# The sample tokens' products with their states: one fp32 product, or two fp32r products over high and low parts

## The chip, the cores and the metric

The kernel runs on one core of one Trainium2 chip. The metric is the device time of one execution in microseconds (us). Engines are named as in the profile: PE (matmul) with its weight loads PEld, DVE (VectorE), ACT (ScalarE), POOL (GpSimd) and SP (SyncE, which issues nearly all DMAs).

## The reference

One inference step of a decoder layer for a prompt of 1024 tokens and for 8 sample tokens, each with its own state. An input projection feeds a gated short convolution (branch A) and a gated delta rule with 8 heads (branch B); both are projected, gated, merged and projected again. What the change touches is the delta rule for the sample tokens, one token for each of 8 samples and 8 heads, with a 128 x 128 state:

```python
Per token: S = a_t S; S = S + beta_t k_t (v_t - k_t^T S); o_t = q_t^T S.
# written for one token, with S the state before it:
r = beta * (v - a * (k^T S))          # k, q are l2-normalised
o = a * (q^T S) + (q^T k) * r
S_new = a * S + k r^T
```

So each head needs k^T S and q^T S for 8 samples: 8 states as weights, each with 2 columns (k and q) that stream past.

## The kernel before

Activations lie with channels on partitions; the 1024 prompt tokens and the 8 sample tokens are 1032 columns, in three groups of 344. A job is one block of 128 output channels of a projection: 3 groups x 8 blocks of the contraction x 3 products. Its operands are fp32 numbers split into a high and a low part of the type fp32r (`xh`, `xl`, `whi`, `wlo`), and high x high, high x low and low x high are summed, each in one pass. `split(hi, lo, src)` makes such parts: a copy on ACT that rounds, and a subtraction on DVE. A head has 6 jobs: k, q, v, two gates, z.

Beside the jobs run strands, written as Python generators: for each head a delta rule over the prompt in 8 chunks (`delta_gen`), and one for the samples (`sample_gen`). A planner (`Sched`) keeps a clock for each engine from assumed costs. After each block of three main products, `slot()` lets every strand whose time has come write its next instructions, up to its next `yield`. So the order on every engine's queue is fixed when the kernel is built; at run time each engine takes its queue in that order and waits where data is missing. PE's queue is main products with the strands' small products strewn in.

In the state chain of `delta_gen`, chunk after chunk, PE forms products with the state S (`S,kq`), DVE forms X from them, PE multiplies (`X,U`), ACT copies the result as `vn`, PE forms `vn,kd`, and DVE adds that to S.

`sample_gen(h)` starts at the first job of head h + 1. It takes slots of 4 KB a partition from `T4` (six of them, shared with other strands and jobs; `T4.ready(n)` asks for n free ones, `T4.get` takes one, `T4.give` returns it), loads the 8 states of the head as `s0` (a DMA of 512 KB on SP's queue), forms the norms of k and q, multiplies the states with k and q, forms r and o, writes r to HBM and reads it back spread over all partitions (`rB`), forms the new states in place and stores them. The trace names the tile of the states S, as it does the state of the chain; `qs_s` holds k and q of all heads and samples.

Of the kernel before, what the change touches and what calls it, by code (L numbers as in the profile page):

```python
# [9 lines left out]
F32R = mybir.dt.float32r  # L10
I32 = mybir.dt.int32
AF = mybir.ActivationFunctionType
ALU = mybir.AluOpType
# [3 lines left out]
P = 128  # L17
D = 1024
NK = 8
S = 1024  # L20
NB = 8
NT = S + NB
NH = 8
C = 128
# [129 lines left out]
def hybrid_step(  # L154
# [9 lines left out]
    V, A, PE, GP, SY = (Paced(e, n, sched) for e, n in (  # L164
        (nc.vector, "V"), (nc.scalar, "A"), (nc.tensor, "PE"), (nc.gpsimd, "GP"), (nc.sync, "SY")))
# [9 lines left out]
    def ps_aux():  # L175
        return psum["pa"].tile([P, 512], F32, tag="pa", name="pa_t")

    def tt(out, a, b, op):
        V.tensor_tensor(out=out, in0=a, in1=b, op=op)

    def ts(out, a, s1, s2=None, op0=ALU.mult, op1=None):
        if s2 is None:
            V.tensor_scalar(out=out, in0=a, scalar1=s1, scalar2=None, op0=op0)
        else:
            V.tensor_scalar(out=out, in0=a, scalar1=s1, scalar2=s2, op0=op0, op1=op1)

    def stt(out, a, s, b, op0, op1):
        V.scalar_tensor_tensor(out=out, in0=a, scalar=s, in1=b, op0=op0, op1=op1)

    def store(out, in_):  # L190
        sched.loose()
        SY.dma_start(out=out, in_=in_)
        sched.loose(False)

    def act(out, in_, func, **kw):
        A.activation(out=out, in_=in_, func=func, **kw)

    def split(hi, lo, src):
        A.copy(out=hi, in_=src)
        tt(lo, src, hi.bitcast(F32), ALU.subtract)  # L200

    def rsqrt(pool, x, n, w, name, tag=""):
        y = pool.tile([P, w], F32, tag=f"rs_y{w}{tag}", name=f"{name}_y")[:n]
        a = pool.tile([P, w], F32, tag=f"rs_a{w}", name=f"{name}_a")[:n]
        ts(y.bitcast(I32), x.bitcast(I32), -0.5, 1597463007.0, ALU.mult, ALU.add)
        for _ in range(3):
            tt(a, y, y, ALU.mult)
            stt(a, a, -0.5, x, ALU.mult, ALU.mult)
            stt(y, a, 1.5, y, ALU.add, ALU.mult)
        return y  # L210
# [49 lines left out]
    qs_s = cpool.tile([P, NH, NB, 2], F32, name="qs_s")  # L260
# [5 lines left out]
    smp = dram.tile([2, NB, NH], F32, name="smp")  # L266
# [10 lines left out]
    def transpose(out, in_):  # L277
        n = in_.shape[0]
        PE.transpose(out, in_, ident[:n, :n])
# [385 lines left out]
    def when(*conds):  # L665
        while not all(c() for c in conds):
            yield
# [124 lines left out]
    flags = {}  # L792
# [413 lines left out]


    def sample_gen(h):
        while not flags.get(("qs", h)) or (h and not flags.get(("smp", h - 1))) or not T4.ready(2):
            yield  # L1210
        sm = lambda name, w=NB: bp.tile([P, w], F32, tag=f"sm_{name}", name=f"sm_{name}")
        s0_, rB_ = T4.get("S0", S), T4.get("rB", S)
        s0 = s0_.rearrange("p (b e) -> p b e", e=C)
        SY.dma_start(out=s0, in_=state_delta[0, :, h].rearrange("b d e -> d b e"))
        kk, qq = qs_s[:, h, :, 0], qs_s[:, h, :, 1]
        prod = sm("prod", 3 * NB).rearrange("p (a b) -> p a b", b=NB)
        tt(prod[:, 0], kk, kk, ALU.mult)
        tt(prod[:, 1], qq, qq, ALU.mult)
        tt(prod[:, 2], kk, qq, ALU.mult)
        yield  # L1220
        pt = ps_aux()
        PE.matmul(pt[:, 0:3 * NB], lhsT=ones, rhs=prod.rearrange("p a b -> p (a b)"), start=True, stop=True)
        s2 = sm("s2", 2 * NB)
        ts(s2, pt[:, 0:2 * NB], EPS, op0=ALU.add)
        qk = sm("qk")
        V.tensor_copy(out=qk, in_=pt[:, 2 * NB:3 * NB])
        rr = rsqrt(bp, s2, P, 2 * NB, "rsk")
        rk_, rq_ = rr[:, 0:NB], rr[:, NB:2 * NB]
        ts(rq_, rq_, C ** -0.5)
        eg_, be_ = gbs[:, 0, :, h], gbs[:, 1, :, h]  # L1230
        ks, fk, fq, egs = sm("ks"), sm("fk"), sm("fq"), sm("egs")
        tt(ks, kk, rk_, ALU.mult)
        tt(fk, rk_, eg_, ALU.mult)
        tt(fq, rq_, eg_, ALU.mult)
        tt(qk, qk, rk_, ALU.mult)
        tt(qk, qk, rq_, ALU.mult)
        V.tensor_copy(out=egs, in_=eg_)
        yield
        pq = ps_aux()
        for b in range(NB):  # L1240
            PE.matmul(pq[:, 2 * b:2 * b + 2], lhsT=s0[:, b, :], rhs=qs_s[:, h, b, :], start=True, stop=True)
            if b % 4 == 3:
                yield
        pqv = pq[:, 0:2 * NB].rearrange("p (n t) -> p n t", t=2)
        r, t_ = sm("r"), sm("t")
        o_ = os_all[:, h, :]
        tt(r, pqv[:, :, 0], fk, ALU.mult)
        tt(r, v_s[:, h, :], r, ALU.subtract)
        tt(r, r, be_, ALU.mult)
        tt(o_, pqv[:, :, 1], fq, ALU.mult)  # L1250
        tt(t_, qk, r, ALU.mult)
        tt(o_, o_, t_, ALU.add)
        yield

        sched.cur.t += 4000.0
        yield
        pt = ps_aux()
        transpose(pt[:NB, 0:P], r)
        rT = bp.tile([NB, P], F32, tag="sm_rT", name="sm_rT")
        V.tensor_copy(out=rT, in_=pt[:NB, 0:P])  # L1260
        SY.dma_start(out=rsc[h], in_=rT)
        rB = rB_.rearrange("p (b e) -> p b e", e=C)
        SY.dma_start(out=rB, in_=rsc[h].unsqueeze(0).to_broadcast([P, NB, C]))
        yield
        for b in range(NB):
            act(rB[:, b, :], rB[:, b, :], AF.Copy, scale=ks[:, b:b + 1])
            stt(s0[:, b, :], s0[:, b, :], egs[:, b:b + 1], rB[:, b, :], ALU.mult, ALU.add)
            if b % 2:
                yield
        store(n_delta_s[0, :, h].rearrange("b d e -> d b e"), s0)  # L1270
        T4.give(s0_)
        T4.give(rB_)
        flags["smp", h] = True
# [85 lines left out]
    for h in range(NH):  # L1359
        i0 = len(jobs)  # L1360
        st_h = head_jobs(h)
        if h:
            hook(i0, lambda h=h: start(sample_gen(h - 1)))
        for g in gates[2 * h:2 * h + 2]:
            gate_job(*g)
        zb_job(h, st_h)
# [3 lines left out]
    for t in range(SG):  # L1370
        branch_a_jobs(t)
    hook(iga, lambda: (start(sample_gen(NH - 1)), start(sample_norm_gen()), start(conv_state_gen("b"))))


# [8 lines left out]
    def alloc(key, side):  # L1383
        pools[key] = tc.alloc_tile_pool(name=key, bufs=1, side=side)
        return pools[key]
# [369 lines left out]
    T4 = Slots(alloc("t4", "left"), "t4", NT4, CY)  # L1755
    bp = tc.alloc_tile_pool(name="bpool", bufs=1, side="left")
# [67 lines left out]
    for j in range(9):  # L1824
        i, n, xr, mh, ml, held = pre.pop(j)
# [33 lines left out]
        for half in range(2):  # L1859
            hs = slice(half * 512, (half + 1) * 512)  # L1860
            stt(yt[:n, hs], yt[:n, hs], r, xr[:n, hs], ALU.mult, ALU.add)
            out = y_prompt[0, i * P:(i + 1) * P, hs] if i < 8 else y_sample[:, 0, hs]
# [38 lines left out]
```

## Time and profile before

| | |
|---|---|
| median of 3 runs | 1423.75 us (1422.88 to 1424.92) |
| profiled execution | 1422.29 us, span 1420.6 us |
| busy in the span | PE 1396.6, PEld 1341.2, DVE 937.7, ACT 658.0, POOL 36.5 us |
| sample products with states | 64 in the program, 128 records in the trace, first at 147.8, last at 776.2 us |
| issue of the 8 state loads | 124.0 (head 0) to 757.6 us (head 7) |

Nearly every instruction is recorded under line L121, where a helper issues them, so groups are told apart by their tiles: `pa_t<-qs_s,S` is a product into `pa_t` with streaming operand `qs_s` and weights S. A row of the timeline has the start in us from the span's start, its length, the engine, the operation, its tiles and shapes, and the number of instructions merged in it; in brackets the idle time ahead of it and what ended it. A row of the groups has the count, then total busy us, mean ns of one, and the idle time just before. A matmul's recorded length contains its way through the array; the distance between starts tells the rate. A row of stretches has its limits, its length, then busy us (and instructions) of PE, PEld, DVE, ACT and POOL, the granted clock of PE, the busy share of the DMA engines, and GB/s.

### The profile page before, as it was taken

The page shows a single profiled execution, that of the slowest core. Times are in us where ns is not written, and L with a number is a line of the kernel's source. Part 1 is how long each engine was busy: PE and PEld are TensorE (multiplying, and loading weights), DVE is VectorE, ACT ScalarE, POOL GpSimd, SP SyncE. Part 2 cuts the span into 40 slices and gives each one's busy share as a digit, 9 for nine tenths or more (in the row PEclk, how much of TensorE's full clock was granted, in tenths as well). Part 3 has the DMA queues.
Part 4 walks back from the last instruction along what each step waited for, and adds up shares of the span by engine and source line. Part 5 has one row for each costly group of instructions (what it writes and reads, how often), then busy time and mean ns, then how long its engine had stood idle before and what let it go on. Part 6 is the DMA issues. An engine that isn't in the chain of part 4 may idle for free.

```text
span 1420.6 us, 25886 instructions
## 1 busy us (share of the span) xinstructions
PE 1396.6 (98%) x10130; PEld 1341.2 (94%) x10130; DVE 937.7 (66%) x2444; ACT 658.0 (46%) x1521; POOL 36.5 (3%) x72
## 2 busy tenths in 40 slices
PE   6999999999999999999999999999999999999997
PEld 4899999999999999999999999999999999999786
DVE  6754846758468494494764816978977857864553
ACT  6767453845529465284573332343333344532211
POOL 0000000000001000010000000000000200000000
PEclk9999999999999999999999999999999999999999
DMA  9523352233323333324232323255621875643221
GB/s 321 147 48 94 91 118 71 80 86 93 87 70 106 87 84 94 72 76 106 62 110 69 85 62 86 95 176 170 207 76 31 248 250 182 231 151 93 95 85 59
DMA packets 191396, 161.76 MB, mean 114 GB/s; under 512 B 34311, under 2 KB 166816, under 8 KB 191266
## 3 DMA queue, kind: packets, MB, share of 16 engines
q1 hardware_dynamic: 186720, 151.58, 36.3%
q0 software_dynamic: 4352, 8.46, 2.0%
q8 instruction: 79, 1.29, 0.4%
q14 instruction: 43, 0.35, 0.1%
q10 hardware_dynamic: 202, 0.08, 0.0%
HBM read 123.40 MB, written 36.91 MB: 113 GB/s over the span
## 4 chain that ended last, share of the span: by engine, by line
PE 91%; DVE 5%; DMA 3%; ACT 1%; SPq 0%; issue 0%; DVEq 0%; ACTq 0%
PE pm_t L121 66%; PE pa_t L121 22%; PE pb L121 2%; DVE kq L121 1%; DMA xs<-in_x_prompt_dram 1%; DMA yraw<-yAsc 1%; DMA wor<-in_w_o_dram 0%; DVE S L121 0%; SPq L121 0%; DMA sg<-gAsc 0%; DVE wlo L121 0%; DVE Tw L121 0%; DVE Ttmp L121 0%; DMA sg<-gBsc 0%; DVE ml L121 0%
## 5 line engine op out<-in xcount | busy, mean ns | idle before, releaser
L121 PE MATMUL pm_t<-xh,whi 128*128 128x344 f32 (+1 forms) x1576 | 520.1, 330 | 0.0
L121 PE MATMUL pm_t<-xl,whi 128*128 128x344 f32 (+1 forms) x1576 | 498.1, 316 | 0.0
L121 PE MATMUL pm_t<-xh,wlo 128*128 128x344 f32 (+1 forms) x1576 | 498.1, 316 | 0.0
L121 PEld LDWEIGHTS pm_t<-xh,whi 128*128 128x128 f32 x1576 | 297.0, 188 | 2.0
L121 PEld LDWEIGHTS pm_t<-xl,whi 128*128 128x128 f32 x1576 | 297.0, 188 | 0.2
L121 PEld LDWEIGHTS pm_t<-xh,wlo 128*128 128x128 f32 x1576 | 296.3, 188 | 0.1
L121 DVE TENSOR_TENSOR wlo<-wraw,whi 128x512 fp32r<-128x512 f32 x136 | 92.0, 687 | 49.6 <-ACT whi L121 49.3
L121 ACT CAST whi<-wraw 128x512 fp32r<-128x512 f32 x136 | 82.7, 624 | 75.9 <-PE pm_t L121 73.3
L121 ACT CAST whi<-wr 128x1024 fp32r<-128x1024 f32 x42 | 44.0, 1047 | 84.6 <-PE pm_t L121 40.7
L121 DVE SCALAR_TENSOR_TENSOR kq<-raw,vecs,kq 128x528 f32<-128x528 f32 x96 | 69.2, 761 | 1.9 <-ACT kq L121 1.9
L121 PE MATMUL pm_t<-thi,wlo 128*128 128x258 f32 x240 | 67.9, 283 | 0.1
L121 PE MATMUL pm_t<-thi,whi 128*128 128x258 f32 x240 | 67.7, 282 | 0.0
L121 PE MATMUL pm_t<-tlo,whi 128*128 128x258 f32 x240 | 67.7, 282 | 0.0
L121 PE MATMUL pa_t<-thi,whi 128*128 128x258 f32 x224 | 64.0, 286 | 1.2 <-ACT whi L121 1.2
L121 PE MATMUL pa_t<-thi,wlo 128*128 128x258 f32 x224 | 64.1, 286 | 0.8 <-DVE wlo L121 0.8
L121 PE MATMUL pa_t<-tlo,whi 128*128 128x258 f32 x224 | 63.7, 285 | 0.0
L121 PE MATMUL pm_t<-yhi,whi 128*128 128x344 f32 x192 | 61.5, 321 | 0.0
L121 PE MATMUL pm_t<-ylo,whi 128*128 128x344 f32 x192 | 61.4, 321 | 0.0
L121 PE MATMUL pm_t<-yhi,wlo 128*128 128x344 f32 x192 | 61.3, 320 | 0.0
L121 DVE TENSOR_TENSOR wlo<-wr,whi 128x1024 fp32r<-128x1024 f32 x42 | 51.2, 1219 | 14.5 <-ACT whi L121 14.5
L121 DVE TENSOR_TENSOR Ttmp<-Tw,At 128x60 f32<-128x60 f32 (+24 forms) x248 | 51.9, 209 | 8.8 <-DMA At<-sA 3.7
L121 ACT ACTIVATE junk<-pa_t 128x128 f32<-128x128 f32 x192 | 53.8, 280 | 5.6 <-PE pa_t L121 2.7
(407 smaller groups left out, 2837.2 us busy)
## 6 DMA issues: line engine op xcount, KB each, us to landing
wraw<-in_w_in_dram SPq DMA_DIRECT2D x60, 512.0 KB
wr<-in_w_in_dram SPq DMA_DIRECT2D x40, 256.0 KB
aw<-in_ada_w_dram SPq DMA_DIRECT2D x16, 512.0 KB
gBsc<-gate SPq DMA_DIRECT2D x8, 516.0 KB
gAsc<-gate SPq DMA_DIRECT2D x8, 516.0 KB
txs<-phi SPq DMA_DIRECT2D x8, 516.0 KB
txs<-plo SPq DMA_DIRECT2D x8, 516.0 KB
tlo<-txs POOLq DMA_DIRECT2D x8, 516.0 KB, 8.1
```

What stands on the lines that cost most here:

```text
L121: r = f(*args, **kw)
```

## The change

`sample_gen` splits the states into `S0h` and `S0l`, and k and q into `sm_qr` (columns k high, q high, k low, q low). For each sample, S0h times all four columns and S0l times the two high ones go into the same place in PSUM, both as fp32r, and the two halves are added on DVE afterwards. The strand waits for three free slots; S0h and S0l are returned after the products, and the slot of rB is taken when it is needed.

```diff
     def sample_gen(h):
-        while not flags.get(("qs", h)) or (h and not flags.get(("smp", h - 1))) or not T4.ready(2):
+        while not flags.get(("qs", h)) or (h and not flags.get(("smp", h - 1))) or not T4.ready(3):
             yield
-        s0_, rB_ = T4.get("S0", S), T4.get("rB", S)
+        s0_, sh_, sl_ = (T4.get(n_, S) for n_ in ("S0", "S0h", "S0l"))
         SY.dma_start(out=s0, in_=state_delta[0, :, h].rearrange("b d e -> d b e"))
+        qr = bp.tile([P, NB, 4], F32R, tag="sm_qr", name="sm_qr")
+        split(qr[:, :, 0:2], qr[:, :, 2:4], qs_s[:, h])
...
         yield
+        hi, lo = (v.bitcast(F32R).rearrange("p (b e) -> p b e", e=C) for v in (sh_, sl_))
+        split(hi, lo, s0)
+        yield
         pq = ps_aux()
         for b in range(NB):
-            PE.matmul(pq[:, 2 * b:2 * b + 2], lhsT=s0[:, b, :], rhs=qs_s[:, h, b, :], start=True, stop=True)
+            PE.matmul(pq[:, 4 * b:4 * b + 4], lhsT=hi[:, b, :], rhs=qr[:, b, :], start=True, stop=False)
+            PE.matmul(pq[:, 4 * b:4 * b + 2], lhsT=lo[:, b, :], rhs=qr[:, b, 0:2], start=False, stop=True)
             if b % 4 == 3:
                 yield
-        pqv = pq[:, 0:2 * NB].rearrange("p (n t) -> p n t", t=2)
+        T4.give(sh_)
+        T4.give(sl_)
+        pqr = pq[:, 0:4 * NB].rearrange("p (n t) -> p n t", t=4)
+        pqv = sm("pq", 2 * NB).rearrange("p (n t) -> p n t", t=2)
+        V.tensor_copy(out=pqv, in_=pqr[:, :, 2:4])
+        tt(pqv, pqr[:, :, 0:2], pqv, ALU.add)
...
+        yield from when(lambda: T4.ready())
+        rB_ = T4.get("rB", S)
```

What stands in the queues is shown at two places. The first is PE at head 0's products, `S_1509` being the tile of head 0's states. Before:

```order
L121 MATMUL pm_t<-xh,wlo 128x344
L121 MATMUL pa_t<-qs_s,S_1509 128x2 x4
L121 MATMUL pm_t<-xh,whi 128x344
L121 MATMUL pm_t<-xl,whi 128x344
L121 MATMUL pm_t<-xh,wlo 128x344
```

With the change, at its place:

```order
L121 MATMUL pm_t<-xh,wlo 128x344
L121 MATMUL pa_t<-sm_qr,S0h 128x4
L121 MATMUL pa_t<-sm_qr,S0l 128x2
L121 MATMUL pa_t<-sm_qr,S0h 128x4
L121 MATMUL pa_t<-sm_qr,S0l 128x2
L121 MATMUL pa_t<-sm_qr,S0h 128x4
L121 MATMUL pa_t<-sm_qr,S0l 128x2
L121 MATMUL pa_t<-sm_qr,S0h 128x4
L121 MATMUL pa_t<-sm_qr,S0l 128x2
L121 MATMUL pm_t<-xh,whi 128x344
```

Four products have become eight in the same burst; heads 0 to 6 have two such bursts each, and head 7's sixteen stand in one.

The second is head 2, whose states are loaded and split while the state chain of head 1 ends (`sz` is the copy of head 2's z job out of PSUM; `on` and `junk,so` take a chunk's output). ACT before:

```order
L121 COPY vn<-pa_t 128x128
L121 ACTIVATE sz<-pm_t 128x344
L121 COPY on<-pa_t 128x128
L121 ACTIVATE junk,so<-pa_t 128x128
L121 COPY vn<-pa_t 128x128
```

ACT with the change:

```order
L121 COPY vn<-pa_t 128x128
L121 CAST S0h<-S_3795 128x1024
L121 ACTIVATE sz<-pm_t 128x344
L121 COPY on<-pa_t 128x128
L121 ACTIVATE junk,so<-pa_t 128x128
L121 COPY vn<-pa_t 128x128
```

The cast of head 2's states stands between the chain's last two vn. DVE at the same place, before:

```order
L121 SCALAR_TENSOR_TENSOR X<-pa_t,nx,vp 128x128
L121 SCALAR_TENSOR_TENSOR S<-S,egl,pa_t 128x128
L121 SCALAR_TENSOR_TENSOR X<-pa_t,nx,vp 128x128
L121 SCALAR_TENSOR_TENSOR S<-S,egl,pa_t 128x128
L121 SCALAR_TENSOR_TENSOR so<-so,ssq 128x8
```

DVE with the change:

```order
L121 SCALAR_TENSOR_TENSOR X<-pa_t,nx,vp 128x128
L121 SCALAR_TENSOR_TENSOR S<-S,egl,pa_t 128x128
L121 TENSOR_TENSOR S0l<-S_3795,S0h 128x1024
L121 SCALAR_TENSOR_TENSOR X<-pa_t,nx,vp 128x128
L121 SCALAR_TENSOR_TENSOR S<-S,egl,pa_t 128x128
L121 SCALAR_TENSOR_TENSOR so<-so,ssq 128x8
```

The subtraction that makes S0l stands between an S and the X that follows it. On SP, head 2's state load stands behind the four stores of `sA` (blocks of the next head's decay matrix) both before and with the change.

## The prediction

> **What bounds the kernel now.** I read the page's engine shares and its chain first, then the busy time by stretch of 80 us with TensorE's waits, then TensorE's groups by form, and last the timeline around one of the 64 products that change.
>
> ```profile
> PE 1396.6 (98%) x10130; PEld 1341.2 (94%) x10130; DVE 937.7 (66%) x2444; ACT 658.0 (46%) x1521; POOL 36.5 (3%) x72
> ...
> PE 91%; DVE 5%; DMA 3%; ACT 1%; SPq 0%; issue 0%; DVEq 0%; ACTq 0%
> ```
> ```profile
> 380.00:460.00 80.00, 79.93 (x621) 77.69 (x619) 55.74 (x181) 44.34 (x114) 3.63 (x4) 1.00 0.34 92
> ...
> sum 720.00, PE 719.39 PEld 702.42 DVE 457.24 ACT 372.91 POOL 17.83; mean PE 79.93 PEld 78.05 DVE 50.80 ACT 41.43 POOL 1.98
> ```
> ```profile
> PE pa_t L121 <- DVE on L121: 0.5, 1, 0.5
> ```
>
> TensorE (PE) carries 91% of the chain. The second fence is the stretch from 140 to 860 us, in which all the changed instructions lie: PE is busy for 719.4 of 720 us at a granted clock of 1.00, while DVE has 457 and ACT 373. The third is the only wait of PE that is listed from 120 to 900 us. So here PE's own instructions are the time: a microsecond taken from its stream is won whole, a wait put into it is lost whole, and work on DVE or ACT costs only where PE ends up waiting for it.
>
> A product here is a weight load (PEld) and a matmul (PE). These are the forms that matter:
>
> ```profile
> L121 PE MATMUL pa_t<-qs_s,S 128*128 128x2 f32 x128 | 15.2, 240 | 0.0
> ```
> ```profile
> L121 PEld LDWEIGHTS pm_t<-xh,whi 128*128 128x128 f32 x1576 | 297.0, 188 | 2.0
> ...
> L121 PEld LDWEIGHTS pa_t<-qs_s,S 128*128 128x128 f32 x128 | 16.0, 191 | 0.0
> L121 PEld LDWEIGHTS pa_t<-ident,kq 128*128 128x128 f32 x128 | 15.2, 140 | 0.8
> ...
> L121 PEld LDWEIGHTS pb<-ahi,cP 128*64 128x64 f32 x36 | 4.1, 134 | 0.2
> ...
> L121 PEld LDWEIGHTS pm_t<-xh,wbh 128*48 128x48 f32 x24 | 2.9, 121 | 2.2 <-ACT last_q L121 1.3
> ```
>
> The 64 fp32 sample products (8 heads of 8 samples) leave 128 records: an fp32 product is two loads and two matmuls, not four. The rows of xh, ahi and wbh are fp32r, with one record for each product. Their loads take 121, 134 and 188 ns at 48, 64 and 128 columns. From 64 to 128 columns that is 54 ns, 0.84 ns a column, so 128 columns occupy about 108 ns and the other 80 ns overlap the neighbours. The fp32 load of as many columns takes 191. The row of ident is that of transposes.
>
> Now the first four sample products of head 0, on PE and on the loads:
>
> ```profile
> 147.61 0.32 PE L121 MATMUL pm_t<-xh,wlo 128*128 128x344 f32 x1
> 147.77 0.95 PE L121 MATMUL pa_t<-qs_s,S 128*128 128x2 f32 x8
> 148.57 0.40 PE L121 MATMUL pm_t<-xh,whi 128*128 128x344 f32 x1
> 148.82 0.32 PE L121 MATMUL pm_t<-xl,whi 128*128 128x344 f32 x1
> ```
> ```profile
> 147.61 1.01 PEld L121 LDWEIGHTS pa_t<-qs_s,S 128*128 128x128 f32 x8
> 148.55 0.19 PEld L121 LDWEIGHTS pm_t<-xh,whi 128*128 128x128 f32 x1
> 148.66 0.19 PEld L121 LDWEIGHTS pm_t<-xl,whi 128*128 128x128 f32 x1
> 148.82 0.19 PEld L121 LDWEIGHTS pm_t<-xh,wlo 128*128 128x128 f32 x1
> ```
> ```profile
> 710.32 23.57 PE pm_t L121 x150
> ```
>
> The last row gives 23.57/150 = 0.157 us for a main product. From 147.61 to 148.82 are 1.21 us, of which two main products take 0.31. The burst of 4 fp32 products therefore costs 0.90 us, 0.112 for each of its 8 loads: with two columns to stream, it is the loads that set the pace. And the fp32r load of xh,whi at 148.55, where nothing long is streaming, lets the next load begin only at 148.66, 0.11 us later. An fp32r load of 128 columns occupies the port as long as an fp32 pass does.
>
> **The change part by part.**
>
> PE, products: removed are 64 fp32 products with 128 loads, added 64 high and 64 low fp32r products with one load each, again 128. Before: 16 bursts of 0.90 = 14.4 us. After: 128 x 0.112 = 14.3. I take 0. The nearest rows bound it: if a load that sets the pace were as short as the transposes' (140 against 188 ns), 128 x 0.048 = 6.1 us would go; if a product of 4 columns had two loads as fp32 has, 14.3 would come.
>
> [...]
>
> ACT and DVE, splits: for each head the state is copied to S0h, S0l is the difference, k and q are split likewise, and the two halves of the result are added. The same operations on the same shapes are in the trace for the prompt's k and q:
>
> ```profile
> L121 ACT CAST kqh<-kq 128x1024 fp32r<-128x1024 f32 x14 | 14.7, 1047 | 3.9 <-DMA gBsc<-gate 2.2 <-DVE S L121 0.7 <-DMA out_dram<-S 0.6
> ...
> L121 ACT COPY last_q<-pm_t 128x11 f32<-128x11 f32 x21 | 3.9, 186 | 0.0
> ```
> ```profile
> L121 DVE TENSOR_TENSOR kql<-kq,kqh 128x1024 fp32r<-128x1024 f32 x14 | 17.0, 1217 | 14.0 <-DMA wraw<-in_w_in_dram 5.5 <-ACT kqh L121 4.8 <-DMA gBsc<-gate 3.1
> ...
> L121 DVE TENSOR_TENSOR vp<-pa_t,vs 128x512 f32<-128x512 f32 x16 | 11.0, 690 | 5.7 <-PE pa_t L121 5.6
> ...
> L121 DVE SCALAR_TENSOR_TENSOR rsk_a<-rsk_a,sm_s 128x16 f32<-128x16 f32 x24 | 4.1, 171 | 0.4
> ```
>
> ACT gets 1.05 us and a small cast (0.19, by last_q) a head, 10 us in all; DVE gets 1.22 and three small ones at 0.17, 1.7 a head, 14 us. Against 347 idle us of ACT and 263 of DVE in the stretch that is covered, and costs nothing by itself. The cover ends where a split stands, in a strict queue, ahead of something that PE needs within a microsecond.
>
> That is so at head 2. The order of the change shows, on ACT, the state's cast between two vn copies of head 1's state chain, and, on DVE, the difference between an S and an X of that chain. The trace of before at that place, SP, DVE and PE:
>
> ```profile
> 301.67 6.33 SPq L121 DMA_DIRECT2D sA<-DB  x4
> 308.10 0.40 SPq L121 DMA_DIRECT2D S<-in_state_delta_dram  x1
> ```
> ```profile
> 310.05 0.35 DVE L121 SCALAR_TENSOR_TENSOR S<-S,egl,pa_t 128x128 f32<-128x128 f32 x1 [2.20 <-PE pa_t L121]
> 311.44 0.35 DVE L121 SCALAR_TENSOR_TENSOR X<-pa_t,nx,vp 128x128 f32<-128x128 f32 x1 [1.05 <-PE pa_t L121]
> 314.00 0.35 DVE L121 SCALAR_TENSOR_TENSOR S<-S,egl,pa_t 128x128 f32<-128x128 f32 x1 [2.20 <-PE pa_t L121]
> ```
> ```profile
> 312.25 0.32 PE L121 MATMUL pm_t<-xh,wlo 128*128 128x344 f32 x1
> 312.41 0.38 PE L121 MATMUL pa_t<-X,U 128*128 128x128 f32 x2
> ```
>
> The load of head 2's state is issued only at 308.10, because SP needs 6.33 us for the four stores ahead of it, and SP's order there is unchanged. How long the load takes is best seen at head 7, where it runs alone:
>
> ```profile
> 757.59 0.37 SPq L121 DMA_DIRECT2D S<-in_state_delta_dram  x1
> ```
> ```profile
> 758.60:759.60 1.00, 1.00 (x9) 1.00 (x8) 0.00 (x0) 0.66 (x2) 0.00 (x0) 1.00 0.24 39
> 759.60:760.60 1.00, 1.00 (x8) 1.00 (x7) 0.00 (x0) 0.00 (x0) 0.00 (x0) 1.00 1.15 348
> 760.60:761.60 1.00, 1.00 (x10) 1.00 (x9) 0.25 (x1) 0.03 (x1) 0.00 (x0) 1.00 0.53 154
> ```
>
> Its 524 KB (39 + 348 + 154 KB moved in these three us) have landed near 761.05, 3.45 us after the issue. Head 2's state then lands at 311.55 at the earliest, the cast ends at 312.6, the difference at 313.8, and X behind it at about 314.2 instead of 311.79. X ended some 0.5 us before X,U's load needed it (0.16 ahead of 312.41), so PE waits 2.4 - 0.5 = 1.9 us; with the load slowed by the stores in front by up to 0.8 us it is 2.7. I take 2.1. The ends are 0 (the load finds the queue free and lands before 309) and 2.7.
>
> At heads 4 and 6 DVE has the difference and one vp (0.69) between S and X, but the state is loaded well ahead: 1.22 + 0.69 fill the 1.05 us for which DVE idled before X and the 0.5 of slack, and 0.37 us is left over, at most 0.7 for both. At heads 3, 5 and 7 the difference stands behind X, where the next S comes 2.56 us later (314.00 - 311.44 at head 2); with two vp the difference takes 2.6 of them, so it mostly fits. For all these I take 0.5, with ends 0 and 1.5.
>
> Queues and slots: no DMA is added or made larger. rB is taken from the slots later, and the strand waits for three free slots instead of two, so that the products come later by a fifth to a half of a job; nothing but the output store and the sample norm follows from them, and the last head's norm still stands six jobs ahead of the point where all strands must be done. The planner prices a sample product at 111 ns now and 217 before, while PE needs the same time, so its clock runs ahead of PE by 0.85 us a head; PE then comes late to what others made ready, which costs nothing.
>
> Sum: 0 + 2.1 + 0.5 = 2.6 us. The profiled execution took 1422.29 us (span 1420.6), so it would take 1424.9; it lies 1.46 below the median of 1423.75, to which the forecast refers: 1426.35, in round 1426.3. About 0.2%, 2.85 us, is what a measurement of this kernel can tell from no change, so this lies just inside it.
>
> **The rivals.** One: the splits cost nothing anywhere. For it: the 1.05 us for which DVE idled before X show that the chain has air at each step, and the order may shift with it. Against: the late issue at 308.10. Time 1423.75; 25%.
>
> Two: fp32r loads are cheap where only loads set the pace, whether by fast loading or because fp32 pays more passes than its records show. For it: the transposes' 140 ns. Against: the 0.11 us between the loads at 148.55 and 148.66. It gives 1426.3 - 6.1 = 1420.2, and is decided when loads of S0h follow each other in under 0.1 us; 6%. [...]
>
> Three, clearly slower: the in-order queues hold PE at every head whose state is loaded shortly ahead of its cast, heads 2, 3, 5 and 7, not at one. It decides where the state lands after the ACT copies ahead of the cast are done:
>
> ```profile
> 576.28 0.37 SPq L121 DMA_DIRECT2D S<-in_state_delta_dram  x1
> ```
> ```profile
> 578.70 0.21 ACT L121 ACTIVATION_READ_ACCUMULATOR junk<-pa_t 128x1 f32 x1
> ...
> 582.11 0.27 ACT L121 COPY vn<-pa_t 128x128 f32<-128x128 f32 x1 [0.99 <-PE pa_t L121]
> ```
>
> At head 5 the state lands at 579.7, 0.8 us after ACT is through, and the cast ends at 580.8, 1.3 us ahead of the next vn. A load slower by 1.5 us uses that up. With 2.1 us at each of four heads: 1423.75 + 8.4 = 1432.2; 15%.
>
> Four: a 4-column fp32r product loads twice, as fp32 does: 1426.3 + 14.3 = 1440.6; 3%, against it the single record of every fp32r form.
>
> **How the numbers follow.** The forecast has 51%; its own range is 1423.5 to 1429 (1.5 for the small heads, 0.6 for the load at head 2, some 0.5 for the stalls that a new order moves about), and half of it lies above 1426.6. Faster by over 0.2% (under 1420.9): 5 of rival two, 3 of one. Slower (over 1426.6): 24 of the forecast, 15 and 3 of three and four. The rest, 50, is within. The range takes in rival one and the lower part of three: 1422.0 to 1430.0.
>
> **What would show it.** In the new trace: loads of S0h and S0l 0.11 us apart, bursts of 8 of them costing 0.90 us (right), or under 0.6 (rival two); 128 records for 128 products (else four). At head 2, ACT idle before the cast of S0h with the state's DMA as releaser, X some 2.4 us later, and a wait of PE of about 2 us for that X; no such wait at heads 3, 5, 7. I am wrong if PE's waits between 140 and 880 us stay as short as before, or if the bursts change their length.

## The result, and the profile after

The changed kernel takes 1430.9 us (median, 1428.84 to 1436.7) against 1423.04 us (1419.97 to 1424.92) for the kernel before on the same chip: ratio 1.0055, 95% interval 1.0041 to 1.0068. It is 7.8 us slower; the forecast was 1426.3, its range ended at 1430.0. The ratios, here and below, compare all runs of a kernel with all runs of the kernel before on the same chip; they differ from the quotient of the two medians by up to 0.07%. The profiled execution has a span of 1429.9 us, 9.3 more than the one before: 6.8 of them lie between the first and the last main product of the jobs, 2.2 behind it.

The engine shares and the chain, then the waits of PE from 120 to 900 us (for each: total us, times, longest):

```profile
PE 1400.3 (98%) x10130; PEld 1342.9 (94%) x10130; DVE 954.6 (67%) x2476; ACT 677.5 (47%) x1547; POOL 37.0 (3%) x72
...
PE 78%; DVE 10%; DMA 7%; ACT 3%; issue 1%; SPq 1%; DVEq 0%; ACTq 0%
```
```profile
PE pa_t L121 <- DVE X L121: 2.9, 1, 2.9
PE pa_t L121 <- DVE on L121: 1.0, 4, 0.4
PE pa_t L121 <- DVE DA L121: 1.0, 1, 1.0
PE pa_t L121 <- DVE S L121: 0.2, 1, 0.2
```

Before, one wait of 0.5 us stood there. The new one is the forecast one, a single wait for X. The groups of the new operations:

```profile
L121 PE MATMUL pa_t<-sm_qr,S0l 128*128 128x2 f32 x64 | 14.7, 250 | 0.0
L121 PE MATMUL pa_t<-sm_qr,S0h 128*128 128x4 f32 x64 | 14.3, 244 | 0.0
L121 PEld LDWEIGHTS pa_t<-sm_qr,S0l 128*128 128x128 f32 x64 | 12.3, 192 | 0.0
...
L121 DVE TENSOR_TENSOR S0l<-S,S0h 128x1024 fp32r<-128x1024 f32 x8 | 9.8, 1221 | 6.9 <-ACT S0h L121 6.9
L121 ACT CAST S0h<-S 128x1024 fp32r<-128x1024 f32 x8 | 8.4, 1047 | 9.3 <-PE pa_t L121 5.0 <-DMA S<-in_state_delta_dram 4.2
```

One record per fp32r product, a load as long as the fp32 one (192 against 191 ns), and the splits at the lengths of kqh and kql. The first burst of head 0, with the main product ahead of it and the two behind it:

```profile
152.03 0.32 PE L121 MATMUL pm_t<-xh,wlo 128*128 128x344 f32 x1
152.19 0.17 PE L121 MATMUL pa_t<-sm_qr,S0h 128*128 128x4 f32 x1
...
153.00 0.40 PE L121 MATMUL pm_t<-xh,whi 128*128 128x344 f32 x1
153.24 0.32 PE L121 MATMUL pm_t<-xl,whi 128*128 128x344 f32 x1
```

From 152.03 to 153.24 are 1.21 us for eight fp32r products, as before for four fp32 ones. Head 2, on SP, ACT, DVE and PE:

```profile
303.55 6.46 SPq L121 DMA_DIRECT2D sA<-DB  x4
310.11 0.40 SPq L121 DMA_DIRECT2D S<-in_state_delta_dram  x1
```
```profile
314.75 1.04 ACT L121 CAST S0h<-S 128x1024 fp32r<-128x1024 f32 x1 [3.72 <-DMA S<-in_state_delta_dram]
```
```profile
311.92 0.35 DVE L121 SCALAR_TENSOR_TENSOR S<-S,egl,pa_t 128x128 f32<-128x128 f32 x1 [2.20 <-PE pa_t L121]
315.82 1.23 DVE L121 TENSOR_TENSOR S0l<-S,S0h 128x1024 fp32r<-128x1024 f32 x1 [3.55 <-ACT S0h L121]
316.97 0.34 DVE L121 SCALAR_TENSOR_TENSOR X<-pa_t,nx,vp 128x128 f32<-128x128 f32 x1
```
```profile
314.12 0.32 PE L121 MATMUL pm_t<-xh,wlo 128*128 128x344 f32 x1
317.37 0.49 PE L121 MATMUL pa_t<-X,U 128*128 128x128 f32 x2 [2.93 <-DVE X L121]
...
318.27 0.49 PE L121 MATMUL pm_t<-xh,whi 128*128 128x344 f32 x1
318.55 0.49 PE L121 MATMUL pm_t<-xl,whi 128*128 128x344 f32 x1
```

The load goes out behind the four sA stores and lands 4.6 us later; the cast, S0l, X and PE's X,U follow one after the other. What the forecast did not have stands in the last two rows: behind the wait the main products start 0.28 us apart instead of 0.157. The stretches there (PE's granted clock is the number behind POOL's):

```profile
314.00:318.00 4.00, 1.07 (x7) 0.79 (x6) 1.49 (x2) 1.94 (x6) 0.00 (x0) 1.00 0.41 117
318.00:322.00 4.00, 4.00 (x19) 4.00 (x18) 1.35 (x7) 1.46 (x7) 0.00 (x0) 0.57 0.05 16
```

From about 318 to 321.5 us the clock is halved. PE's queue in the run "e2_split_late" below, which has no wait here, is the same row by row. From 276 to 331 us (two main products of the same place in the queue) the change needs 4.79 us more than that run: 3.10 in the step at X,U, 1.7 in the slow products behind it.

### The profile page after: what moved, and what is told of

It is laid out like the page before. It is cut to its first block, busy times and chain, and to the rows that moved or that the text cites. A ratio compares the mean times of both kernels' runs of the same rounds, so it can differ in the third digit from the quotient of the medians.

```text
span 1429.9 us, 25946 instructions
## 1 busy us (share of the span) xinstructions
PE 1400.3 (98%) x10130; PEld 1342.9 (94%) x10130; DVE 954.6 (67%) x2476; ACT 677.5 (47%) x1547; POOL 37.0 (3%) x72
## 4 chain that ended last, share of the span: by engine, by line
PE 78%; DVE 10%; DMA 7%; ACT 3%; issue 1%; SPq 1%; DVEq 0%; ACTq 0%
PE pm_t L121 57%; PE pa_t L121 19%; DVE acc L121 2%; PE pb L121 2%; DVE kq L121 1%; DMA gcB<-gsc 1%; DVE wlo L121 1%; SPq L121 1%; DMA xs<-in_x_prompt_dram 1%; DMA aw<-in_ada_w_dram 1%; DMA yraw<-yAsc 1%; DVE Tw L121 1%; DVE Ttmp L121 1%; DMA wor<-in_w_o_dram 0%; DVE wr L121 0%
## 5 line engine op out<-in xcount | busy, mean ns | idle before, releaser
L121 DVE TENSOR_TENSOR wlo<-wr,whi 128x1024 fp32r<-128x1024 f32 x42 | 51.2, 1218 | 13.8 <-ACT whi L121 13.7
```

Of the source, the lines that this page charges most:

```text
L121: r = f(*args, **kw)
```

## The experiments

The theory: the loss is the queue at head 2 (the wait for X and the half clock, 4.8 us), with the products at no cost and about 3 us elsewhere. The rivals: the work of the splits on ACT and DVE all over the program; fp32r products dearer than fp32 ones. Where an edit leaves instructions out, the planner is still told their costs, so that the order stays close to the change's.

### Where head 2's load is issued (e1_load_elsewhere)

```diff
+        if h == 2:
+            sched.dma("SY", 4 * NB * C * P)
+            GP._e.dma_start(out=s0, in_=state_delta[0, :, h]...)   # POOL's queue
+        else:
             SY.dma_start(out=s0, in_=state_delta[0, :, h]...)
```

> The change, with the load of head 2's states alone issued from POOL's queue in place of SP's, so that it stands behind none of the four sA stores; on ACT and DVE the cast and S0l then stand a few rows earlier, ahead of the last X of head 1's chain, with their data there. Theory 'queue at head 2': PE's wait of 2.9 us for X and the stretch of 0.57 granted clock behind it both go, 3.1 + 1.7 = 4.8 us; the kernel stays about 3 us above before: 1426 us (1424.5 to 1427.5), granted clock 1.00 from 314 to 322 us. Rival 'the work of the splits': 0.9 + 1.2 us a head on ACT and DVE, all over the program, costs the 7.8 us, and where one load is issued changes nothing: 1430 to 1431 us. Rival 'fp32r products cost more than fp32': 1430 to 1431 us too.

Measured: 1442.24 us, ratio 1.0126 (1.0112 to 1.0140), slower than the change. POOL's issue, ACT's cast, and PE's wait:

```profile
312.48 1.02 POOL L1216 DMA_DIRECT2D S<-in_state_delta_dram  x1 [37.26 <-DMA sA<-DB]
```
```profile
319.55 1.04 ACT L121 CAST S0h<-S 128x1024 fp32r<-128x1024 f32 x1 [15.13 <-DMA S<-in_state_delta_dram]
```
```profile
PE pa_t L121 <- ACT vn L121: 12.8, 1, 12.8
```

The edit did not do what it was meant for. The load waited on POOL too, until 312.48, the trace names an sA store as what released it, and it took 7 us to land. The cast now stood one row earlier, ahead of vn, and PE waited 12.8 us. The theory's 1426 us was missed, and so were both rivals' 1430 to 1431: by the ratios this one load, landing later with its cast one row earlier, moved the time by 10 us. What the load waited for besides SP's queue stays open.

### Head 2's split behind its norms (e2_split_late, e11_split_late_again)

```diff
+        if h == 2:      # makes the cast follow the norms' s2
+            V._e.tensor_copy(out=sh_[:, 0:NB].bitcast(F32R), in_=s2[:, 0:NB])
         split(hi, lo, s0)
```

> The change, with head 2's cast made to follow head 2's own norms (a small DVE copy from the norms into the cast's destination ahead of it), so that cast and S0l come some 15 us later, behind head 1's chain; the load stays late on SP's queue, PE's queue is the same row by row. Theory 'queue at head 2': the wait for X and the half clock go although the load is as late as before, 4.8 us: 1426 us (1424.5 to 1427.5). If it is the late load or its collision with the stores that costs time by itself, and not what stands behind the cast: 1430 to 1431 us. The rivals on the work of the splits and on the products: 1430 to 1431 us.

> Head 2's split behind its norms, once more, so that it stands beside the two others on one chip. Before: ratio 1.0023 (1.0011 to 1.0034). If the 3.2 us that it left are real, the ratio is again at or above 1.0015; if it was a high draw, it lies at 1.001, which the profile's 2 us between the first and the last main product would give.

Measured: 1426.65 us, ratio 1.0023 (1.0011 to 1.0034), and again 1427.77, 1.0017 (1.0006 to 1.0027). In the first, the cast starts at 325.10, and the stretches at head 2 are full:

```profile
312.00:316.00 4.00, 4.00 (x30) 4.00 (x29) 0.70 (x2) 0.88 (x6) 0.00 (x0) 1.00 0.88 249
316.00:320.00 4.00, 4.00 (x28) 4.00 (x27) 3.53 (x21) 3.99 (x13) 0.00 (x0) 1.00 0.06 16
320.00:324.00 4.00, 4.00 (x28) 4.00 (x27) 3.93 (x8) 3.98 (x5) 0.00 (x0) 1.00 0.53 131
```

No wait, clock 1.00. With the same work (and one small copy more), the same load on the same queue and the same queue of PE, 1.0055 falls to 1.0020 (mean of two), 5.0 us: the 4.8 of the trace. That the cast stands ahead of the chain is what costs.

### Splits without the products, and one product (e3_splits_only, e4_one_product)

```diff
-            PE.matmul(pq[:, 4*b:4*b+4], lhsT=hi[:, b, :], rhs=qr[:, b, :], ...)
-            PE.matmul(pq[:, 4*b:4*b+2], lhsT=lo[:, b, :], rhs=qr[:, b, 0:2], ...)
+            PE._e.matmul(pq[:, 4*b:4*b+2], lhsT=s0[:, b, :], rhs=qs_s[:, h, b, :], ...)   # e3
+            PE.matmul(pq[:, 4*b:4*b+4], lhsT=hi[:, b, :], rhs=qr[:, b, :], ...)            # e4
```

> The splits, the slots and the order of the change stay, but the products are the fp32 ones of before again (k and q times the unsplit states; S0h, S0l and the split k and q are made and not used by PE). Theory 'queue at head 2', in which the fp32r products cost what the fp32 ones do: 1430.9 us again (1429.5 to 1432), with the wait for X of about 3 us at head 2 and the half clock. Rival 'fp32r products cost more than fp32': most of the 7.8 us goes, 1423 to 1426 us.

> The change without the 64 products of S0l (the low part of the states is made and left out of the sum): one fp32r product per sample. Splits, load and queue at head 2 stay. Theory 'queue at head 2' with each 128-column load at 0.112 us on PE's path: 64 x 0.112 = 7.2 us less than the change, 1423.7 us (1422.5 to 1425), the wait for X and the half clock still there. Rival: the loads lie beside other work, and their number costs nothing: 1430 to 1431 us. Rival 'fp32r products cost more than fp32' (say 0.17 us each): 1420 us or less.

Measured: with the fp32 products 1432.91 us, 0.9 above the range expected, ratio 1.0055 (1.0040 to 1.0071), that of the change. PE's wait at head 2, and the clock there:

```profile
PE pa_t L121 <- DVE X L121: 4.3, 1, 4.3
```
```profile
314.00:318.00 4.00, 0.42 (x2) 0.43 (x3) 1.49 (x2) 1.82 (x5) 0.00 (x0) 0.74 0.47 133
318.00:322.00 4.00, 4.00 (x17) 4.00 (x17) 0.73 (x4) 1.28 (x6) 0.00 (x0) 0.50 0.04 13
322.00:326.00 4.00, 4.00 (x25) 4.00 (x24) 3.43 (x19) 3.37 (x11) 0.00 (x0) 0.90 0.01 4
```

The equal ratio alone doesn't show much, since its interval reaches some 2 us to each side. Head 2 costs 6.9 us in this trace, 2.1 more than in the change, since the wait is longer and the half clock lasts from 315.9 to 322.8 us, twice as long. With head 2 taken out, the two traces agree within 0.5 us from the first to the last main product (869.9 and 870.3 us), and a burst with its two main products takes 1.21 us in both. So the kind of product costs nothing that shows. With one product 1423.28 us, 0.9997 (0.9987 to 1.0007), 8.3 us below the change by the ratios where 7.2 were expected, with its wait for X still at 2.9. A burst of four samples there:

```profile
335.40 0.32 PE L121 MATMUL pm_t<-xh,wlo 128*128 128x344 f32 x1
335.56 0.50 PE L121 MATMUL pa_t<-sm_qr,S0h 128*128 128x4 f32 x4
335.92 0.40 PE L121 MATMUL pm_t<-xh,whi 128*128 128x344 f32 x1
336.16 0.32 PE L121 MATMUL pm_t<-xl,whi 128*128 128x344 f32 x1
```

From 335.40 to 336.16 are 0.76 us, where eight loads needed 1.21: 0.45 for four, 0.112 each, 7.2 for the 64. An fp32r load of 128 columns costs as much here as one of the two loads of an fp32 product (0.112 us in both), and what won on PE was to have fewer.

### No splits (e5_slots_only, e12_slots_only_again), and before once more (e8_before_again)

```diff
-        split(hi, lo, s0)          # and the fp32 products as in e3
+        sched.note("A", ...); sched.note("V", ...)     # the planner's prices stay
```

> The change without the splits of the states: no cast, no S0l, the fp32 products of before; the three slots, the late slot of rB, the split of k and q, the two extra small DVE instructions a head and the order that the planner makes for the change stay. It asks where the 3.2 us lie that were left with head 2's split moved away (1426.65 against 1424.37 us). Theory 'queue at head 2': no wait for X, granted clock 1.00 at 318 us. If the rest comes from the splits' work on ACT and DVE, it is gone too: 1424 us (1423 to 1425, the level of before on the same chip); if it comes from the slots and the order, 1427 us (1426 to 1428).

> No splits of the states, fp32 products, slots and order of the change, once more. Before: ratio 1.0003 (0.9991 to 1.0014), though its profile was 3.3 us longer than before's between the first and the last main product. If the order alone costs what that profile shows, the ratio is 1.0015 to 1.0025; if the splits cost what is left, 0.9995 to 1.001.

> The kernel before once more, for a second profile: how far PE's waits outside head 2 differ between two executions of one kernel. If the change's waits of 0.3 to 1 us at head 0 and behind 900 us are variation from run to run, waits of that size move about here too; if they are the change's, this profile has the same waits as the first of before: none over 0.2 us between 120 and 170 us, and 2.2 us for whi, wlo and cP behind 900 us.

Measured: 1426.07 us, ratio 1.0003 (0.9991 to 1.0014), and 1425.94, 1.0008 (0.9998 to 1.0018). PE's waits for `on`, of the second of these and of before once more:

```profile
PE pa_t L121 <- DVE on L121: 1.8, 4, 1.0
```
```profile
PE pa_t L121 <- DVE DA L121: 0.5, 1, 0.5
PE pa_t L121 <- DVE on L121: 0.5, 1, 0.5
```

Without splits too, PE waits four times for `on` where the kernel before waits once, in both its profiles: that comes with the order. The longest of these waits (1.0 us here, 1.6 in the first run) stands behind a wait of DVE for rB from ACT, 0.8 and 1.4 us long. The wait for DA at head 0 (1.0 us in the change) is there with 0.5 us in the second profile of before and not in the first, and behind 900 us before's own listed waits went from 2.2 to 3.6 us: that much is variation.

The two ways of measuring the rest don't agree. From the first to the last main product of the jobs (by their starts in the traces) before needs 868.3 and 868.8 us, the change 875.1, head 2's split late 870.4 twice, no splits 872.0 and 870.5. About 1.5 of the 872.0 are a stretch of half clock from 787.3 to 790.7 us, where PE has no listed wait:

```profile
784.00:788.00 4.00, 4.00 (x29) 3.83 (x30) 2.29 (x17) 0.58 (x3) 0.00 (x0) 0.91 0.02 5
788.00:792.00 4.00, 4.00 (x23) 3.71 (x23) 2.47 (x12) 1.88 (x6) 0.00 (x0) 0.66 0.01 4
```

So in these traces 1.8 to 2 us are left without head 2 and without that stretch, with splits or without. By the ratios no splits cost 0.4 and 1.1 us and late splits 3.3 and 2.4, and the second run's 1.0008 lies where the expectation put the case that the splits cost what is left. The intervals of the two kinds overlap, and behind the last main product the traces differ among themselves (490.6 and 491.9 us in the two of before, 490.1 to 493.7 in the others). Whether the splits cost a microsecond or two away from head 2 stays open.

### How much of the split (e6_split_eighth)

```diff
-        split(hi, lo, s0)
+        A._e.copy(out=hi[:, 0], in_=s0[:, 0])                       # one state in eight
+        V._e.tensor_tensor(out=lo[:, 0], in0=s0[:, 0], in1=hi[:, 0]..., op=ALU.subtract)
```

> The change with one state in eight split: cast and S0l are 128x128 instead of 128x1024, and all products of a head take the first sample's parts as weights, so PE's loads and products are the same in number, and the other seven states' parts are left out. ACT still waits at head 2 for the load; S0l stands one row earlier on DVE, ahead of the chain's S. Cast and S0l shrink by 0.85 and 1.1 us, and S is done after them: X comes about 1 to 1.5 us sooner, so PE's wait is 1.4 to 2 us instead of 2.9. Theory 'the half clock follows a wait of about 3 us': it does not come behind this shorter wait, so 1 to 1.5 and 1.7 us go, 1428 us (1426.5 to 1429). If any wait of PE brings it: 1429.5 to 1430. Rival 'the work of the splits': nearly all of it is gone, 1424 us.

Measured: 1431.91 us, ratio 1.0049 (1.0031 to 1.0066); the expected 1428 was missed. PE's wait and the clock:

```profile
PE pa_t L121 <- DVE S L121: 3.7, 2, 3.5
```
```profile
312.00:316.00 4.00, 0.51 (x5) 0.22 (x3) 0.55 (x2) 0.94 (x5) 0.00 (x0) 1.00 0.61 172
316.00:320.00 4.00, 4.00 (x18) 4.00 (x19) 0.35 (x1) 0.41 (x3) 0.00 (x0) 0.62 0.12 30
```

S0l, one row earlier on DVE, held the chain's S and not only X, so PE stopped earlier, at S,kq, and for longer; head 2 costs 5.3 us here. With seven eighths of the splits' work gone nearly all of the loss is still there: it hangs on when the load lands, not on how long the split takes. The rival 'work of the splits' falls as the main cause.

### Only S0l late, and all splits late (e9_low_late, e10_all_late)

```diff
-        split(hi, lo, s0)                                            # e9
+        A.copy(out=hi, in_=s0)
+        if h == 2:
+            V._e.tensor_copy(out=sl_[:, 0:NB].bitcast(F32R), in_=s2[:, 0:NB])
+        tt(lo, s0, hi.bitcast(F32), ALU.subtract)
```
```diff
+        V._e.tensor_copy(out=sh_[:, 0:NB].bitcast(F32R), in_=s2[:, 0:NB])   # e10, every head
         split(hi, lo, s0)
```

> The change with only S0l of head 2 moved behind the norms (a small DVE copy from the norms into S0l ahead of it); the cast stays where it is on ACT, between the chain's last vn and the copies behind it, and waits there for the load. PE's queue is the same row by row. X is then free to go at about 312.5 us; ACT frees vn only behind the cast, sz, on and junk, at about 316.6 us, when PE has gone on to the main products before vn,kd at 315.3: a wait of 1.2 to 1.6 us in place of 2.9. Theory: a wait this short leaves the clock at 1.00, so 1.5 + 1.7 = 3.2 us less than the change: 1427 to 1428 us, ratio 1.0025 to 1.0035. If any wait brings the half clock: 1.5 us less, ratio 1.0045. If ACT's block costs PE as much as DVE's: ratio 1.0055.

> The splits of all eight heads behind the norms of their heads, in place of head 2's alone; PE's queue is the same row by row, the full change otherwise. With head 2's moved, two waits stay at head 1 that a kernel without splits does not have, 0.30 us at 233 and 0.23 us at 246 us, both of PE for the chain's S behind S0l on DVE. Theory 'the rest is such collisions': these go, 0.5 us, and what else the splits still cost at the other heads: ratio to before 1.0003 to 1.0018, 1 us or more below the run with head 2 alone. If the rest is not in where the splits stand: ratio 1.0023 as there.

Measured for S0l: 1431.4 us, ratio 1.0046 (1.0030 to 1.0062). DVE was free, and ACT's cast alone held vn:

```profile
PE pa_t L121 <- ACT vn L121: 2.2, 1, 2.2
```
```profile
314.00:318.00 4.00, 1.93 (x13) 1.65 (x12) 0.00 (x1) 1.86 (x6) 0.00 (x0) 1.00 0.54 144
318.00:322.00 4.00, 3.82 (x18) 3.82 (x19) 2.64 (x15) 3.02 (x11) 0.00 (x0) 0.66 0.05 16
322.00:326.00 4.00, 4.00 (x25) 4.00 (x25) 4.00 (x12) 3.97 (x9) 0.00 (x0) 0.91 0.46 110
```

A wait of 2.2 us also brought the half clock, so "about 3 us" as the point where it comes falls; the ratio is the 1.0045 that was expected if a short wait brings it too. Here the place costs 4.07 us: 2.4 in the step at vn,kd, 1.7 behind it.

All splits late: 1429.08 us, 1.0026 (1.0014 to 1.0038), no better than head 2's alone. PE's waits for S are gone, but those for `on` grew:

```profile
PE pa_t L121 <- DVE on L121: 3.8, 2, 2.0
```

Ahead of these two `on` DVE waits 1.76 and 1.55 us for rB from ACT, and behind the first of them the clock is halved again (443.0 to 446.4 us). From the first to the last main product the trace takes 874.1 us, against 870.4 with head 2's alone late. So moving every split doesn't win the rest: what the waits for S gave back, `on` at other heads lost.

### A version faster than both (e7_one_product_late)

Head 2's cast is late as in e2_split_late, and the product of S0l is left out as in e4_one_product, here with S0l itself.

```diff
+        if h == 2:
+            V._e.tensor_copy(out=sh_[:, 0:NB].bitcast(F32R), in_=s2[:, 0:NB])
-        split(hi, lo, s0)
+        A.copy(out=hi, in_=s0)
-            PE.matmul(pq[:, 4*b:4*b+2], lhsT=lo[:, b, :], rhs=qr[:, b, 0:2], ...)
```

> Two parts put together: one fp32r product a sample (the 64 products of S0l and S0l itself left out, so the low part of the states is left out of the sum), and head 2's cast behind head 2's norms. Theory 'queue at head 2' with loads at 0.112 us: 1423.3 us as measured for one product, less 4.8 us for the wait and the half clock: 1418.5 us (1417 to 1420), ratio to before 0.996. If the two gains share a cause they don't add: 1421 to 1423 us.

Measured: 1420.5 us against 1425.29, ratio 0.9965 (0.9953 to 0.9977); the time is 0.5 above the range expected, the ratio close to the expected 0.996. The two gains add: 0.9997 falls by 0.0032, 4.6 us. It is faster than both kernels, at the price of the low part of the states.

## Why the prediction was wrong

**What bounds the kernel:** right. PE stays at 98%, and the time followed PE's waits.

**Products at 0:** right. A burst of eight loads still takes 1.21 us with its two main products, with fp32 products instead nothing is won that shows, and each load left out gives 0.112 us. Rivals two and four fall: these fp32r loads follow each other 0.112 us apart, as the fp32 ones of before do.

**Head 2:** place and mechanism right, row by row; the term of 2.1 us with its end of 2.7 is the step that failed. It was 4.8. Two things are in it:

- The landing. The step took 3.45 us from head 7's load, and gave up to 0.8 more for the stores in front, the author's estimate. From issue to the start of the cast it was 4.6 us in the change, 4.4 in e4_one_product, 5.5 in e3_splits_only, e6_split_eighth and e9_low_late. The 1.9 us worked out at 3.45 and the 1.2 us that the load came later make the 3.1 us of PE's step at X,U; the end of 2.7 was too low. In the trace of before the DMA engines stood idle in the two us ahead of the issue of head 7's load and were 0.72 and 0.89 busy ahead of head 2's. That this delays the load would fit, but no run shows it.
- The clock. The step priced PE's wait and not what follows it, 1.7 us at half clock. The trace of before had such a place, behind waits of 1.2 and 0.8 us for weights, and the prediction passed over it:

```profile
1160.00:1164.00 4.00, 2.02 (x11) 1.60 (x11) 2.09 (x3) 4.00 (x5) 0.00 (x0) 0.88 0.13 53
1164.00:1168.00 4.00, 4.00 (x26) 4.00 (x26) 2.85 (x5) 0.74 (x1) 0.00 (x0) 0.70 0.13 17
```

Landing and clock together would have made the sum 1423.75 + 4.8 + 0.5 = 1429.

**The other heads, 0.5 with an end of 1.5:** too small. About 1.8 us lie in the trace between the first and the last main product away from head 2, part of it waits for `on` that come with the new order, without any split. "PE then comes late to what others made ready, which costs nothing" was wrong by that; which part of the change makes the order cost this (the planner's prices, the third slot, rB's later slot) no run separates. By the ratios it is 2.4 to 3.3 us; the difference is not located.

**Rival three** gave 1432.2, nearest to what was measured, by another mechanism: heads 3, 5 and 7 have no wait for X; one head was held, and it cost more than twice its term.

## What to carry to other kernels

A helper that waits for a DMA must not stand, in an in-order queue, ahead of a chain that the bounding engine needs; moving the cast of one head behind work that depends on the same head won 5.0 us of 7.8 with nothing else changed but a small copy. Price a wait put into a dense PE stream as the wait plus what the half clock costs behind it (here 1.7 us behind waits of 2.2 to 3.5 us, 2.5 behind 4.3), and look in the trace of before for stretches with a granted clock under 1 to see how short a wait already brings one. Where few columns stream, count weight loads and not products: here two fp32r products in place of one fp32 product were two loads in place of two, 0.112 us each as before.

## What the runs showed of the hardware

The stretch at half clock was as long behind a wait of 2.2 us (e9_low_late, from 319.3 to 322.7 us) as behind one of 2.9 (the change, 318.1 to 321.5) or 3.5 (e6_split_eighth, 317.0 to 320.4): 3.4 us. Behind 4.3 us (e3_splits_only) it was 6.8, behind 12.8 (e1_load_elsewhere) 13.7 us, two and four times as long. It began 3.6 us after PE went idle in the change (at 314.44 us) and 4.5 us after it in e6_split_eighth (at 312.50), so not at a fixed distance behind the start of the wait. In the change's trace the next one begins at 1171.4 us, 853.3 us after the one at 318.1, which is 250 times the length of 3.413 us (318.075 to 321.488); in the trace of before two begin 252.6 us apart (1163.0 and 1415.6 us), 74 times that length.

So the length of a wait alone didn't decide. In e10_all_late a wait of 1.98 us brought the half clock and one of 1.84 us didn't; waits of 1.2 and 0.8 us close together brought it in the trace of before, and 1.4 and 0.8 us at the same place in e5_slots_only didn't; and there it came once with no listed wait. Behind 12.8 us of waiting PE was at half clock from the start:

```profile
316.00:320.00 4.00, 0.00 (x0) 0.00 (x0) 0.00 (x0) 0.45 (x1) 0.00 (x0) 0.50 0.59 141
320.00:324.00 4.00, 2.84 (x12) 2.84 (x13) 1.58 (x3) 1.64 (x6) 0.00 (x0) 0.50 0.00 0
```
